# A decoder layer on one core: bank pairs in the other order, the first quarter of x in halves, and banks of their own for the first FFN products

## The chip, the cores and the metric

The kernel runs on one core of a Trainium2 chip. A core has five engines with a queue each: TensorE (PE in the profile, its weight loads PEld), VectorE (DVE), ScalarE (ACT), GpSimd (POOL) and SyncE (SP), which here only issues DMAs. PE multiplies from SBUF into PSUM, which has eight banks of 128 x 512 floats. The metric is the device time of one execution in microseconds. Before the change three runs took 2125.6, 2127.41 and 2127.95 us, a median of 2127.41.

## What is computed

One layer with sparse attention, then a gated feed-forward network (FFN), on x of 512 tokens by 2048 channels in float32:

```python
hn = rmsnorm(x, mix_norm_g)
h = x + nsa_mixer(hn, ...)                 # 16 heads of 128, 4 key/value groups
h = h + swiglu(rmsnorm(h, ffn_norm_g), ffn_w_in, ffn_w_out)   # D_FF = 5632
return rmsnorm(h, final_norm_g)

def nsa_mixer(h, ...):
    proj = h @ w_in                        # q, kc, vc, ks, vs, kw, vw, gates
    ...                                    # compressed, selected and window branches
    o = gates0 * o_c + gates1 * o_s + gates2 * o_w
    return o @ w_out

def swiglu(h, w_in, w_out):
    z = h @ w_in
    a, b = z[..., :D_FF], z[..., D_FF:]
    return (jax.nn.silu(a) * b) @ w_out
```

## The kernel before

**Products.** Every float32 operand is split into a high and a low part (`hi`, `lo`, or a trailing `_h`, `_l`), and a product is three matmuls (`three`, L267 to L269): high by high, high by low, low by high. Making the parts costs one copy on ACT and one subtraction on DVE for each tile: L97 and L98 for weights, L402 and L403 for x.

**Order.** The order of instructions on each engine is that of the Python program; the framework adds the semaphores. An engine works its queue in order, so an instruction that waits holds all behind it. A pool of PSUM or SBUF that is closed gives its place to the next pool opened there, and the first write to such a place waits until the old tile was read for the last time.

**Weights.** `Weights` (L81 to L98) streams granules of 128 x 1024 floats: `load` issues the DMA into one of three `raw` buffers, `split` makes `whi` and `wlo` (four buffers each), `ahead(n)` splits up to n granules past those taken and loads up to three more, `take` hands one out. Its DMAs go on SP's queue, and on POOL's while the heads run.

**The start (L372 to L485).** x comes as four tiles of 128 tokens, each in four quarters of 512 channels. SP loads a weight granule and the even tiles of a quarter, ACT's queue the odd tiles of the first two quarters, and SP all of the last two. PE meanwhile transposes the identity `N_WARM` = 24 times. Then the 16 blocks of the first quarter are transposed (L452) into four banks, ACT and DVE turn each of four banks into `hn_h[k]` and `hn_l[k]` (`scaled_in`), and eight steps follow: `ws` yields after each `three` for one half u of the columns and one channel block k. ACT's squares (L408) and the next quarter's transposes (`chunk`, L398) are mixed in, chunk 4 after step five. This goes on for the four quarters, with q from 0 to 3.

**Bank pairs.** The projections of stage 1 take their two banks in turn from `psx` (2 banks) and `ps1` (6 banks, under three names), by `proj_tiles`. The last pair of the stage is the q of heads 0 and 1 (`q_out`: DVE reads the bank at L319, ACT and DVE write `qh`, `ql` at L292, L293). Then stage 2 opens `ps2` in the place of `ps1`: a score tile of three banks (`s`), one bank for the values (`o`) and two more for projections; its own pairs come in turn from `psx` and `ps2`, beginning with `psx`.

**The heads.** `scores(h, t)` makes the scores of head h and token tile t into the one score tile, takes the maxima (DVE, L800) and the exponentials (ACT, L802). `finish` scales and transposes them in blocks and writes them to DRAM (`d_p`, L817); `fetch` brings them back transposed (`ptr`, L821); `turn` splits them (L838, L842), and `values` multiplies them by v into `o`. Between these steps `pump(h, step)` draws dense work, the projections of later heads, from one stream: steps of 650 ns by the plan's own count (three matmuls of 512 columns) until the count reaches a goal that rises by 20800 ns for each head of twelve steps. The lead in the goal is four steps. Ahead of head 0 there are four calls, one behind each of its scores, at steps 9, 10, 11 and 11.7 of the head before.

**From attention to the FFN.** `out_tiles` and the norms use `psx` and `ps3` (6 banks). Then three plain column blocks of the FFN (N_PLAIN, tiles `pp` of `ps3`), each followed by its gate (`plain_out`: ACT's silu, L1068, or DVE's product, L1066). Then `early` closes both pools and `pf` opens: f0 to f3, two banks each. From there `products(q)` makes seven half-size products per unit (first into f0), and `merge(p)` sums them (L1155 to L1165). After the last unit the second weight matrix follows in units of two row blocks: `W2.take` splits weights, `split_a` the gated activations (`thi`, `tlo`, L1227, L1008), which come from DRAM through buffers `rawx` and `tt` (L1222).

Of the kernel before, what the change touches and what calls it, by code (L numbers as in the profile page):

```python
# [10 lines left out]
F32 = mybir.dt.float32  # L11
# [27 lines left out]
TP_GAP, HN_GAP = 40, 48  # L39
RESYNC = 14  # L40
PT_STEP = 224
SPREAD, N_WARM = UL, 24


def _bucket_onehot():
# [128 lines left out]
def nsa_block(ctx: ExitStack, tc: tile.TileContext, x, rel_bias, mix_g, ffn_g, fin_g, w_in, w_out,  # L174
# [9 lines left out]
    dram = ctx.enter_context(tc.tile_pool(name="dram", bufs=1, space=DRAM))  # L184
    front, early = ctx.enter_context(ExitStack()), ctx.enter_context(ExitStack())
    hnp = front.enter_context(tc.tile_pool(name="hnp", bufs=1))
    psx = early.enter_context(tc.tile_pool(name="psx", bufs=2, space=PSUM))
    specs, specs2, marks, off = granules(w_in, w1k, w1v, w_out, f_in, f_out)
    W = Weights(nc, rawp, convp, specs)
    W.at, W.off = 48, off  # L190
# [159 lines left out]
    with ExitStack() as st1:  # L350
# [2 lines left out]
        turns = iter(range(1000))  # L353

        def proj_tiles(n=2):
            return [(ps1 if next(turns) % 4 > 1 else psx).tile([128, 512], F32, name="proj") for _ in range(n)]

        c0p = st1.enter_context(tc.tile_pool(name="c0p", bufs=1))
        posT = c0p.tile([128, 2, 32], F32, name="posT")
# [2 lines left out]
        with ExitStack() as st0:  # L362
# [7 lines left out]
            ones = xp.tile([128, 128], F32, name="ones")  # L370
            diag = xp.tile([128, NT, 128], F32, name="diag")
            nc.scalar.dma_start(g16, mix_g.rearrange("o (k p) -> (o k) p", p=128))  # L372
            for q in range(4):
                if q < RAW:
                    W.load()
                for t in range(NT):
                    eng = nc.scalar if q < 2 and t % 2 else nc.sync
                    eng.dma_start(xt[t][:, 512 * q:512 * (q + 1)], x[tok(t), 512 * q:512 * (q + 1)])
                if q == 0:
                    act(warm, epsc, AF.Sqrt)  # L380
                if q == 1:
                    nc.sync.dma_start(oh, onehot[:, :UL])
            pool.dma_start(pos[:, 0], pos_k)
# [61 lines left out]
            p = bank([128, KC])  # L445
            nc.tensor.transpose(p, g16, ident[:KC, :KC])
            dve.tensor_copy(gcol, p)
            W.split()
            ps = [bank([128, S]) for _ in range(4)]
            for t in range(NT):  # L450
                for k in range(4):
                    nc.tensor.transpose(ps[k][:, tok(t)], xt[t][:, 128 * k:128 * (k + 1)], ident)  # L452
            for k in range(4):
                scaled_in(k, ps[k])
            ps = proj_tiles()
            for q in range(4):
                it = ws(ps, q, W.take(0))
                next(it)
                if q == 3:
                    factors()  # L460
                W.ahead(1)
                if q == 1:
                    pos_turn()
                    table(0, 512)
                    table(512, UL)
                if q == 2:
                    by_blocks()
                for i in ((0, 1), (2, 3, 4), (5, 6, 7), ())[q]:
                    square(i)
                for _ in range(4):  # L470
                    next(it)
                if q == 3:
                    W.ahead(2)
                for k in range(4 * q + 4, 4 * q + 8):
                    if q < 3:
                        chunk(k)
# [153 lines left out]
    with ExitStack() as st2:  # L630
# [112 lines left out]
        STEPS = 12  # L743

        def pump(h, step):
            at = h + (step + 4) / STEPS
            goal = 20800 * min(at, 13) + 22500 * max(at - 13, 0)
            while done["ns"] < goal:
                c = next(stream, "end")
                if c == "end":  # L750
                    return
                done["ns"] += c or 0
# [118 lines left out]
        for i in range(4):  # L871
            scores(0, 3 - i)
            if i > 1:
                fetch(5 - i, pool)
            if i:
                finish(0, 4 - i)
            pump(-1, min(9 + i, 11.7))
        for h in range(H):
            seq = [(b, kt) for kt in (3, 2, 1, 0) for b in (0, 1)] + [(-1, 0)]
            for i in range(STEPS):  # L880
# [34 lines left out]
    n2_hl = hn_t  # L915
    resid = ctx.enter_context(ExitStack())
    accp = resid.enter_context(tc.tile_pool(name="accp", bufs=1))
    ps3 = early.enter_context(tc.tile_pool(name="ps3", bufs=4, space=PSUM))
    acc = accp.tile([128, NT, D], F32, name="acc")
    spill = 256 * N_SPILL  # L920
    nc.sync.dma_start(acc[:, :, spill:], x[:, spill:].rearrange("(t p) c -> p t c", p=128))
# [18 lines left out]
    with tc.tile_pool(name="n2", bufs=1) as n2:  # L940
# [25 lines left out]
        for t in range(NT):  # L966
# [93 lines left out]

    def plain_out(p, ps):
        E[p] = ep.tile([128, 6, 256], F32, name="E")
        for u in range(2):
            o = gate_out(p)[:, 512 * u:512 * (u + 1)]
            if p % 2:
                dve.tensor_tensor(o, gate_out(p - 1)[:, 512 * u:512 * (u + 1)], ps[u], op=OP.mult)  # L1066
            else:
                act(o, ps[u], AF.Silu)  # L1068
        if p % 2:
            keep_a(p)  # L1070

    def keep_a(p):
        pool.dma_start(d_a[p // 2], gate_out(p))
# [49 lines left out]
    def products(q):  # L1123
        p, u = q // 2, q % 2
        if not u:
            banks[p] = [pf.tile([128, 512], F32, name=f"f{i}").rearrange("p (a c) -> p a c", a=2)
                        for i in range(4)]
# [40 lines left out]
    with tc.tile_pool(name="tmp", bufs=1) as tmp:  # L1168
        todo = sums(tmp)

        def some(n):
            for _ in range(n):
                next(todo, None)

        for i in range(4):
            run(ws(pa, i, gs[i], 256, 512, start=False, of=n2_hl))
            W.ahead(min(i + 1, 3))
            some(1 if i < 3 else 2)
        for p in range(N_PLAIN):
            if p:  # L1180
                pa = [ps3.tile([128, 512], F32, name="pp") for _ in range(2)]
                for i in range(4):
# [8 lines left out]
                    run(ws(pa, i, w, of=n2_hl))  # L1191
            W.ahead(3)
            plain_out(p, pa)
# [91 lines left out]
    merge(NQ // 2 - 1)  # L1285
    front.close()

# [129 lines left out]
            yield  # L1417

    w8, todo = [], iter(())
    n, na, pending = 0, 1, None  # L1420
    for b in range(4):
        units = ORDER[b][:-N_TAIL] if b == 3 else ORDER[b]
        po = [pf.tile([128, 512], F32, name=f"f{i}") for i in range(4)]
        qs = {x: pf.tile([128, 512], F32, name=f"f{i}") for i, x in enumerate(("p1", "p5", "p6", "p7"))}
# [84 lines left out]
```

## Time and profile before

| | before |
|---|---|
| three runs, us | 2125.6, 2127.41, 2127.95 |
| the profiled execution, us | 2127.83 |
| its span, us | 2126.1 |
| mean granted clock of PE | 0.997 |
| matmuls | 14697 |
| DMA, MB | 388.08, mean 183 GB/s |

The span is that of the instructions on the core; the execution's time has 1.7 us around it. In the rows that follow, a row of the timeline has its start, its length, engine, line, operation, the tile written and those read, and in brackets how long the engine had stood idle before and what released it. A matmul's length overlaps the next one's, so the distance of two starts says what one costs: 0.23 us for 512 columns. A row of windows has the stretch, its length, the busy time of PE, PEld, DVE, ACT and POOL with counts, the granted clock of PE (1.00 is full), the busy share of the DMA engines and GB/s.

```profile
PE   9999999999999999999999999999999999999998
DVE  5565777877786466898888888888888777877785
PEclk9999999999999999999999999999999999999999
DMA  7555667666676633444344343443333776878894
```

These are the busy tenths of the span in 40 slices of 53 us. The start is in the first slice, the passage from stage 1 to the heads in the fourth, that to the FFN's products in the seventeenth, and that to the second weight matrix in the thirty-second.

### The profile page before, as it was taken

The numbers are of one execution on the slowest core, as the hardware profiler recorded it, in microseconds if no ns is written. First come the engines' busy times: TensorE is split into PE (matmuls) and PEld (weight loads), VectorE is DVE, ScalarE is ACT, GpSimd is POOL, SyncE is SP. The second block draws the span as 40 slices with busy tenths as digits, with TensorE's granted clock in tenths as the row PEclk, the third lists the DMA queues.
The fourth block names the chain that finished last, engine by engine and source line by source line (L and its number), as shares of the span: only waits on it lengthen the run. The fifth ranks groups of instructions, "written<-read, shape, count | busy, mean of one in ns | idle before, by whom it ended". The sixth has DMA issues, their size and how long they took to land.

```text
span 2126.1 us, 37171 instructions
## 1 busy us (share of the span) xinstructions
PE 2099.3 (99%) x14697; PEld 1947.6 (92%) x14697; DVE 1634.5 (77%) x2670; ACT 932.5 (44%) x1447; POOL 125.8 (6%) x206
## 2 busy tenths in 40 slices
PE   9999999999999999999999999999999999999998
PEld 7898788898989889899999999999999888999996
DVE  5565777877786466898888888888888777877785
ACT  5344455555554334434334343443434444444344
POOL 1000111111111000000000000000000000001000
PEclk9999999999999999999999999999999999999999
DMA  7555667666676633444344343443333776878894
GB/s 228 180 151 151 192 193 201 184 200 188 199 233 203 240 140 109 128 131 129 120 129 129 120 126 123 129 127 122 123 124 122 273 274 213 302 271 309 307 335 143
DMA packets 272635, 388.08 MB, mean 183 GB/s; under 512 B 34155, under 2 KB 204715, under 8 KB 271820
## 3 DMA queue, kind: packets, MB, share of 16 engines
q1 hardware_dynamic: 247660, 279.19, 41.7%
q0 software_dynamic: 22896, 102.31, 13.9%
q10 hardware_dynamic: 1904, 4.20, 0.5%
q8 instruction: 115, 1.88, 0.4%
q14 instruction: 60, 0.49, 0.1%
HBM read 320.52 MB, written 70.36 MB: 184 GB/s over the span
## 4 chain that ended last, share of the span: by engine, by line
PE 68%; DVE 1%; DMA 1%; ACT 1%; issue 0%; ACTq 0%; DVEq 0%
PE f L268 19%; PE f L269 19%; PE f L267 19%; PE proj L267 2%; PE proj L269 2%; PE proj L268 2%; PE pp L267 1%; PE pp L269 1%; PE pp L268 1%; PE po L267 1%; PE po L268 1%; PE po L269 1%; DMA tt<-d_a 1%; PE pp L245 0%; DVE tlo L1008 0%
## 5 line engine op out<-in xcount | busy, mean ns | idle before, releaser
L98 DVE TENSOR_TENSOR wlo<-raw,whi 128x1024 fp32r<-128x1024 f32 (+1 forms) x226 | 270.8, 1200 | 114.5 <-ACT whi L97 114.3
L97 ACT ACTIVATE whi<-raw 128x1024 fp32r<-128x1024 f32 (+1 forms) x226 | 234.4, 1040 | 222.6 <-DVE raw L1008 123.7
L1008 DVE TENSOR_TENSOR tlo<-tt,thi 128x1536 fp32r<-128x1536 f32 (+2 forms) x135 | 197.2, 1460 | 109.2 <-ACT thi L1110 87.2
L267 PE MATMUL f<-hn_h,whi 128*128 128x256 f32 x984 | 272.0, 276 | 0.8 <-ACT E L1068 0.8
L268 PE MATMUL f<-hn_l,whi 128*128 128x256 f32 x984 | 271.9, 276 | 0.0
L269 PE MATMUL f<-hn_h,wlo 128*128 128x256 f32 x984 | 271.9, 276 | 0.0
L1105 ACT ACTIVATE whi<-raw 128x1024 fp32r<-128x1024 f32 x123 | 126.0, 1057 | 293.7 <-DVE raw L1008 283.5
L267 PE MATMUL proj<-hn_h,whi 128*128 128x512 f32 x512 | 204.3, 399 | 0.5 <-ACT hn_h L402 0.5
L268 PE MATMUL proj<-hn_l,whi 128*128 128x512 f32 x512 | 200.9, 392 | 0.3 <-DVE hn_l L403 0.3
L269 PE MATMUL proj<-hn_h,wlo 128*128 128x512 f32 x512 | 200.7, 392 | 0.0
L267 PEld LDWEIGHTS f<-hn_h,whi 128*128 128x128 f32 x984 | 184.8, 188 | 1.2 <-ACT E L1068 1.2
L269 PEld LDWEIGHTS f<-hn_h,wlo 128*128 128x128 f32 x984 | 184.7, 188 | 0.0
L268 PEld LDWEIGHTS f<-hn_l,whi 128*128 128x128 f32 x984 | 184.7, 188 | 0.0
L1110 ACT ACTIVATE thi<-tt 128x1536 fp32r<-128x1536 f32 x82 | 121.9, 1486 | 82.7 <-PE f L268 71.1
L269 PE MATMUL proj<-whi,hn_l 128*128 128x256 f32 (+2 forms) x496 | 146.3, 295 | 2.9 <-DVE hn_l L703 2.9
L1008 DVE TENSOR_TENSOR wlo<-raw,whi 128x1024 fp32r<-128x1024 f32 x123 | 147.1, 1223 | 1.1 <-ACT whi L1105 1.1
L267 PE MATMUL proj<-whi,hn_h 128*128 128x256 f32 (+2 forms) x496 | 146.6, 296 | 0.8 <-ACT hn_h L702 0.8
L268 PE MATMUL proj<-wlo,hn_h 128*128 128x256 f32 (+2 forms) x496 | 145.7, 294 | 0.0
L269 PE MATMUL f<-whi,tlo 128*128 128x512 f32 x320 | 125.0, 391 | 0.6 <-DVE tlo L1008 0.6
L268 PE MATMUL f<-wlo,thi 128*128 128x512 f32 x320 | 125.1, 391 | 0.3 <-DVE wlo L98 0.3
L267 PE MATMUL f<-whi,thi 128*128 128x512 f32 x320 | 124.8, 390 | 0.0
L269 PEld LDWEIGHTS proj<-hn_h,wlo 128*128 128x128 f32 x512 | 96.5, 189 | 21.5 <-DVE wlo L98 0.2
(327 smaller groups left out, 6104.7 us busy)
## 6 DMA issues: line engine op xcount, KB each, us to landing
raw<-in_ffn_w_in SPq DMA_DIRECT2D x135, 512.0 KB, 3.6
raw<-in_ffn_w_out SPq DMA_DIRECT2D x88, 512.0 KB, 6.0
rawx<-in_ffn_w_in SPq DMA_DIRECT2D x41, 512.0 KB, 4.9
rawx<-d_a SPq DMA_DIRECT2D x31, 512.0 KB, 4.9
ah<-d_s POOLq DMA_DIRECT2D x16, 896.0 KB, 7.2
al<-d_s POOLq DMA_DIRECT2D x16, 896.0 KB, 9.5
raw<-in_nsa_w_in SPq DMA_DIRECT2D x24, 512.0 KB, 4.6
raw<-in_nsa_w_in POOLq DMA_DIRECT2D x24, 512.0 KB, 4.8
```

The source lines that it names most:

```text
L97: self.nc.scalar.activation(hi[:, :n], src, AF.Copy)
L98: self.nc.vector.tensor_tensor(lo[:, :n], src, hi[:, :n].bitcast(F32), op=OP.subtract)
L267: mm(o, ah, bh, start=start, stop=False, skip_group_check=True)
L268: mm(o, ah, bl, start=False, stop=False, skip_group_check=True)
L269: mm(o, al, bh, start=False, stop=stop, skip_group_check=True)
L1008: dve.tensor_tensor(o, a, b, op=OP.subtract)
L1105: act(h, r, AF.Copy)
L1110: act(h, ttf, AF.Copy)
```

## The change

- **Start.** The first granule and the first quarter of x are loaded, split, transposed and multiplied in halves of 256 channels: `half(0)`, two steps, `half(1)`, six steps. The odd tiles of the second quarter move from ACT's queue to SP's. `N_WARM` falls from 24 to 20.
- **Bank pairs.** `proj_tiles` gives `ps1` where it gave `psx`, and the other way round.
- **Lead.** In `pump` the lead is five steps up to head 0 and falls evenly to four at head 3. The four calls ahead of head 0 are at steps 8, 9.3, 10.6 and 11.9.
- **FFN banks.** `psx` is closed by itself after the last norm and `pf0` opens in its place, for f0; `ps3` lies at the other end of PSUM, and `pf` has f1 to f3. The gate of a plain block is made half by half, as soon as that half's last matmul is issued (`end`), and the next weights are split ahead of the second half.
- **Last merge.** The second unit's weights and activations are split ahead of the last `merge`, and the loop begins with `na` = 2.

```diff
-SPREAD, N_WARM = UL, 24
+SPREAD, N_WARM = UL, 20
...
-    psx = early.enter_context(tc.tile_pool(name="psx", bufs=2, space=PSUM))
+    firstp = ctx.enter_context(ExitStack())
+    psx = firstp.enter_context(tc.tile_pool(name="psx", bufs=2, space=PSUM))
...
-            return [(ps1 if next(turns) % 4 > 1 else psx).tile([128, 512], F32, name="proj") for _ in range(n)]
+            return [(psx if next(turns) % 4 > 1 else ps1).tile([128, 512], F32, name="proj") for _ in range(n)]
...
-            for q in range(4):
+            first = rawp.tile([128, 1024], F32, name="raw")
+            for a in range(2):
+                w0 = slice(512 * a, 512 * (a + 1))
+                nc.sync.dma_start(first[:, w0].rearrange("p (k c) -> p k c", k=2), specs[0][2][0][2][:, 2 * a:2 * a + 2])
+                for t in range(NT):
+                    eng = nc.scalar if t % 2 else nc.sync
+                    eng.dma_start(xt[t][:, 256 * a:256 * (a + 1)], x[tok(t), 256 * a:256 * (a + 1)])
+                if not a:
+                    act(warm, epsc, AF.Sqrt)
+            W.nd = 1
+            for q in range(1, 4):
                 if q < RAW:
                     W.load()
                 for t in range(NT):
-                    eng = nc.scalar if q < 2 and t % 2 else nc.sync
-                    eng.dma_start(xt[t][:, 512 * q:512 * (q + 1)], x[tok(t), 512 * q:512 * (q + 1)])
-                if q == 0:
-                    act(warm, epsc, AF.Sqrt)
+                    nc.sync.dma_start(xt[t][:, 512 * q:512 * (q + 1)], x[tok(t), 512 * q:512 * (q + 1)])
...
-            W.split()
-            ps = [bank([128, S]) for _ in range(4)]
-            for t in range(NT):
-                for k in range(4):
-                    nc.tensor.transpose(ps[k][:, tok(t)], xt[t][:, 128 * k:128 * (k + 1)], ident)
-            for k in range(4):
-                scaled_in(k, ps[k])
+            W.ncv = W.nt = 1
+            whi, wlo = (convp.tile([128, 1088], F32R, name=f"w{n}")[:, W.at:W.at + 1024] for n in ("hi", "lo"))
+
+            def half(a):
+
+                c = slice(512 * a, 512 * (a + 1))
+                act(whi[:, c], first[:, c], AF.Copy)
+                dve.tensor_tensor(wlo[:, c], first[:, c], whi[:, c].bitcast(F32), op=OP.subtract)
+                p2 = [bank([128, S]) for _ in range(2)]
+                for t in range(NT):
+                    for k in range(2):
+                        nc.tensor.transpose(p2[k][:, tok(t)], xt[t][:, 128 * (2 * a + k):128 * (2 * a + k + 1)], ident)
+                for k in range(2):
+                    scaled_in(2 * a + k, p2[k])
+
+            def first_steps(ps):
+                for a in range(2):
+                    for i in range(4):
+                        u, k = i // 2, 2 * a + i % 2
+                        cs = slice(256 * k + 128 * u, 256 * k + 128 * (u + 1))
+                        three(ps[u], whi[:, cs], wlo[:, cs], hn_h[:, k], hn_l[:, k], k == 0, False)
+                        yield
+                        if not a and i == 1:
+                            half(1)
+
+            half(0)
             ps = proj_tiles()
             for q in range(4):
-                it = ws(ps, q, W.take(0))
-                next(it)
+                it = ws(ps, q, W.take(0)) if q else first_steps(ps)
+                for _ in range(1 if q else 3):
+                    next(it)
...
-                for _ in range(4):
+                for _ in range(4 if q else 2):
                     next(it)
...
-            at = h + (step + 4) / STEPS
+            at = h + step / STEPS
+            at += (4 + min(max(1 - at / 3, 0), 1)) / STEPS
...
-            pump(-1, min(9 + i, 11.7))
+            pump(-1, 8 + 1.3 * i)
...
-    ps3 = early.enter_context(tc.tile_pool(name="ps3", bufs=4, space=PSUM))
+    ps3 = early.enter_context(tc.tile_pool(name="ps3", bufs=4, space=PSUM, side="right"))
...
+        firstp.close()
+        pf0 = ctx.enter_context(tc.tile_pool(name="pf0", bufs=2, space=PSUM))
         pa = [ps3.tile([128, 512], F32, name="pp") for _ in range(2)]
...
+    def f_tile(i):
+        return (pf if i else pf0).tile([128, 512], F32, name=f"f{i}")
...
         products(q)
+    W2.ahead(2)
+    split_a(1)
     merge(NQ // 2 - 1)
...
-    n, na, pending = 0, 1, None
+    n, na, pending = 0, 2, None
```

More of the change, by code (lines that the diff above doesn't have):

```diff
@@ L1062, in plain_out, with end @@
         E[p] = ep.tile([128, 6, 256], F32, name="E")
-        for u in range(2):
+        def end(u):
             o = gate_out(p)[:, 512 * u:512 * (u + 1)]
@@ L1068, in plain_out @@
                 act(o, ps[u], AF.Silu)
-        if p % 2:
-            keep_a(p)
+            if p % 2 and u:
+                keep_a(p)
+        return end
     def keep_a(p):
@@ L1125, in products @@
         if not u:
-            banks[p] = [pf.tile([128, 512], F32, name=f"f{i}").rearrange("p (a c) -> p a c", a=2)
-                        for i in range(4)]
+            banks[p] = [f_tile(i).rearrange("p (a c) -> p a c", a=2) for i in range(4)]
         order = ("p1", "p5", "p2", "p3", "p7", "p6", "p4") if p else ("p1", "p5", "p2", "p7", "p6", "p4", "p3")
@@ L1173, in some @@
                 next(todo, None)
+        end = plain_out(0, pa)
         for i in range(4):
-            run(ws(pa, i, gs[i], 256, 512, start=False, of=n2_hl))
+            run(ws(pa, i, gs[i], 256, 512, start=False, end=end, of=n2_hl))
             W.ahead(min(i + 1, 3))
@@ L1181, in nsa_block @@
                 pa = [ps3.tile([128, 512], F32, name="pp") for _ in range(2)]
+                end = plain_out(p, pa)
                 for i in range(4):
@@ L1190, in nsa_block @@
                         load_unit(2)
-                    run(ws(pa, i, w, of=n2_hl))
+                    run(ws(pa, i, w, end=end, of=n2_hl))
             W.ahead(3)
-            plain_out(p, pa)
         for u in range(2):
@@ L1419, in nsa_block @@
     w8, todo = [], iter(())
-    n, na, pending = 0, 1, None
+    n, na, pending = 0, 2, None
     for b in range(4):
         units = ORDER[b][:-N_TAIL] if b == 3 else ORDER[b]
-        po = [pf.tile([128, 512], F32, name=f"f{i}") for i in range(4)]
-        qs = {x: pf.tile([128, 512], F32, name=f"f{i}") for i, x in enumerate(("p1", "p5", "p6", "p7"))}
+        po = [f_tile(i) for i in range(4)]
+        qs = {x: f_tile(i) for i, x in enumerate(("p1", "p5", "p6", "p7"))}
         first7 = next(j for j in units if j in SEVEN[b])
```

## The prediction

> **What bounds the kernel.** I read the page first (busy time, then the chain that ended last), then the waits of PE, then the timeline around each wait.
>
> ```profile
> PE 2099.3 (99%) x14697; PEld 1947.6 (92%) x14697; DVE 1634.5 (77%) x2670; ACT 932.5 (44%) x1447; POOL 125.8 (6%) x206
> PE 68%; DVE 1%; DMA 1%; ACT 1%; issue 0%; ACTq 0%; DVEq 0%
> ```
>
> PE is busy for 99% of the span, and no other engine has a visible share of the chain. The change takes no matmul of the model away, so it can win only where PE stands still. The waits of PE are few enough to count (engine, tile and line, released by: us in total, times, longest):
>
> ```profile
> PE o L267 <- issue: 3.0, 1, 3.0
> PE proj L269 <- DVE hn_l L703: 2.9, 2, 2.2
> PE s L267 <- DVE yt L319: 1.7, 1, 1.7
> PE tr L452 <- DMA x<-in_x: 1.6, 2, 0.9
> ```
>
> Of these, the second (the reload of heads near 600 us) is not touched: from head 3 on the new lead is the old one, four steps. The other three are addressed, and five waits of 1 us or less whose rows come with their parts. A wait is worth a little more than its idle time, since a matmul after a gap no longer overlaps the one before; below I take starts: the gap between two starts less the usual pitch, 0.23 us for 512 columns and 0.12 for 256 or for the small ones.
>
> **1. The start.** Before:
>
> ```profile
> 1.42 4.56 PE L444 MATMUL tr<-ident 128*128 128x128 f32 x24 [1.42 <-POOL ident masks.py:199]
> 8.79 0.33 PE L452 MATMUL tr<-ident,x 128*128 128x128 f32 x1 [0.61 <-DMA x<-in_x]
> 10.31 0.75 DVE L403 SCALAR_TENSOR_TENSOR hn_l<-tr,gcol,hn_h 128x512 fp32r<-128x512 f32 x1 [2.82 <-ACT hn_h L402]
> 10.33 0.50 PE L267 MATMUL proj<-hn_h,whi 128*128 128x512 f32 x1 [0.45 <-ACT hn_h L402]
> 14.47 0.60 PE L398 MATMUL tr<-ident,x 128*128 128x128 f32 x4
> GB/s 0 0 0 140 207 236 343 312 164 234 388 399 395 378 379 364 376 369 376 365 244 284 348 367 386 382 386 386 396 389 393 377 367 348 347 350 333 121 247 350
> ```
>
> The last row is the DMA view of the first 24 us, 0.6 us a slice. It gives 0.84 MB by 5.4 us and 0.98 MB by 6.0. The first half needs 0.79 MB (0.26 of the granule, 0.52 of x), and the ACT queue mixes some of its second halves in, so I put it at 5.6 to 6.0. From the last tiles' arrival to the first matmul went 10.33 - 8.79 = 1.54 us; with half the transposes I take 1.1, so the first matmul starts near 7.0, not 10.33. DVE's 0.75 us per hn_l holds the first two steps to 8.9; the eight transposes of the second half take 0.9; steps three to five take 3 x 0.69, hn_l[2] and hn_l[3] arriving just ahead. Transposes of chunk 4 come at 11.9 instead of 14.47: 2.57 us. They also need the second quarter of x: 3.15 MB with the two granules, which the row reaches at 12.0. I take 2.2. Bounds: 2.57, and 0 if that quarter lands as late as 14.47 (the trace shows only that it was there by then). The odd tiles of the second quarter change from ACT's queue to SP's, behind granule 1; that is in the 3.15 MB. Later quarters are not needed before q = 1.
>
> The four warm-up transposes removed (24 took 4.56 us) cost nothing, since PE waits for x anyway; if that cover fails it is the clock that is late, a rival below. ACT's two squares of q = 0 still come between hn_h[3] and hn_h[4]; hn_h[4] is needed only in q = 1, some 3.9 us after chunk 4's transposes.
>
> *A rule against it.* The first 24 us move at up to 399 GB/s with DMAs of 256 and 512 KB in flight together. The Trainium skill, "DMA: Bandwidth & Descriptors", Bandwidth, asks for DMAs of 1 MiB and gives 0.95 us for 64 KB against 6.15 us for 1 MB, so about 0.6 us fixed for each DMA, my estimate from the two; five more DMAs would be 3 us if they ran one after the other, and the start would win nothing. Here several queues overlap them, so I don't follow it.
>
> **2. Bank pairs, and more filling behind the first scores.**
>
> ```profile
> 200.56 0.69 DVE L293 TENSOR_TENSOR ql<-yt,qh 128x512 fp32r<-128x512 f32 x1 [0.70 <-ACT qh L292]
> 202.65 0.68 DVE L319 SCALAR_TENSOR_TENSOR yt<-proj,ybc 128x512 f32<-128x512 f32 x1
> 204.03 0.69 DVE L293 TENSOR_TENSOR ql<-yt,qh 128x512 fp32r<-128x512 f32 x1 [0.70 <-ACT qh L292]
> 205.31 0.19 DVE L800 CUSTOM_DVE_ANT_0 cx<-s,biasc 128x31 f32<-128x31 f32 x1 [0.58 <-PE s L269]
> ...
> 201.37 0.39 PE L269 MATMUL proj<-hn_h,wlo 128*128 128x512 f32 x1
> 203.48 0.37 PE L267 MATMUL s<-k0h,qh 128*128 128x288 f32 x1 [1.72 <-DVE yt L319]
> 213.25 0.40 PE L267 MATMUL s<-k0h,qh 128*128 128x288 f32 x1 [0.78 <-DVE mx L800]
> 219.18 0.28 PE L269 MATMUL s<-k0h,ql 128*128 128x256 f32 x1
> 222.50 0.30 PE L267 MATMUL o<-pth,v0h 128*128 128x128 f32 x1 [3.05 <-issue]
> ...
> 212.49 19.49 SPq L817 DMA_DIRECT2D d_p<-p  x17
> 217.09 0.77 POOL L821 DMA_DIRECT2D ptr<-d_p  x1 [17.07 <-DMA d_p<-p]
> 222.10 0.51 ACT L838 ACTIVATE pth<-ptr 128x128 fp32r<-128x128 f32 x2 [4.23 <-DMA ptr<-d_p]
> ```
>
> Head 0's q was ready at 201.25 (first row); the scores waited until 203.48 for DVE's read of head 1's bank, because the score tile lies on ps1's banks. With the pairs turned, that last pair is in psx, and the scores start at 201.6: 2.11 - 0.23 = 1.88 us. But DVE's maxima still stand behind the second ql (204.03 to 204.72), so they start only 0.6 earlier than 205.31; the second scores, which overwrite what the maxima read, then make PE wait about 1.0 us. From there the softmax chain is some 0.9 us earlier (0.6 on DVE, and the rest since it then waits less for PE). The wait at 213.25 (0.78 idle) goes, filled by one extra step. The long one is a chain through DRAM: write at 212.49, fetch at 217.09, ACT at 222.10. Its 9.6 us I leave, so the values start near 221.6. Meanwhile, by the goals of pump, 16 steps of 0.69 have been done rather than 14. Together 0.9 + 2 x 0.69 = 2.25; I take 2.2. Bounds: all three gaps gone, 1.88 + 0.78 + 3.20 = 5.9; and -0.7, if the granule that the ninth step loads, now ahead of the second fetch on POOL's queue, holds the chain by its 0.52 MB at 246 GB/s (2.1 us; the rate is in the rows below), with the 1.4 of the steps kept. What is late next is the same fetch, with a gap of about 2.85 us. The first steps now write psx just after its own last pair; its first bank had been read before 200.56, so nothing waits. The lead given up by head 3 moves work, and adds none.
>
> *The clock.* After that gap the clock falls:
>
> ```profile
> 222.00:224.00 2.00, 1.50 (x6) 1.26 (x7) 1.39 (x7) 0.51 (x2) 0.42 (x2) 0.86 0.91 306
> 224.00:226.00 2.00, 2.00 (x8) 1.63 (x7) 1.29 (x6) 0.56 (x2) 0.68 (x1) 0.50 0.83 246
> 226.00:228.00 2.00, 2.00 (x8) 1.64 (x8) 1.05 (x4) 1.75 (x7) 0.00 (x0) 0.79 0.67 205
> ...
> 611.98 0.39 PE L269 MATMUL proj<-whi,hn_l 128*128 128x256 f32 x1 [2.15 <-DVE hn_l L703]
> 613.00:615.00 2.00, 2.00 (x10) 1.89 (x10) 0.69 (x8) 1.80 (x8) 0.00 (x0) 0.50 0.83 224
> ```
>
> The granted clock is the seventh figure: 2 x (0.14 + 0.50 + 0.21) = 1.7 us lost. At 612 a gap of 2.15 us did the same, so I expect 2.85 to do it too and count nothing. The Trainium skill, "TensorE: Matmul & The Clock Gate", Part 1, has a free-running window of 3.4 us and half the clock after an idle one; by that a gap of 2.85 would keep the clock. The trace disagrees with it at 2.15.
>
> **3. Own first banks in the FFN.**
>
> ```profile
> 879.15 0.39 PE L269 MATMUL pp<-hn_h,wlo 128*128 128x512 f32 x1
> 880.31 0.39 PE L267 MATMUL f<-hn_h,whi 128*128 128x256 f32 x1 [0.77 <-ACT E L1068]
> ```
>
> 1.16 - 0.23 = 0.93 us. The first product now writes pf0, on psx's idle banks; its 12 matmuls cover 1.37 us, and ACT's gate, still ending about 880.3, frees the others. The gates themselves are issued earlier, but ACT reaches the last no sooner. Bounds 0 and 0.93; I take 0.9.
>
> **4. The second unit's splits before the last merge.**
>
> ```profile
> 1661.68 1.14 DVE L1011 TENSOR_TENSOR E<-E,f 128x512 f32<-128x512 f32 x2 [2.08 <-ACT E L1155]
> 1665.93 1.22 DVE L98 TENSOR_TENSOR wlo<-raw,whi 128x1024 fp32r<-128x1024 f32 x1
> 1667.07 1.22 DVE L1008 TENSOR_TENSOR tlo<-tt,thi 128x1024 fp32r<-128x1024 f32 x1
> ...
> 1666.52 0.39 PE L267 MATMUL f<-whi,thi 128*128 128x512 f32 x1
> 1667.20 0.50 PE L268 MATMUL f<-wlo,thi 128*128 128x512 f32 x1 [0.29 <-DVE wlo L98]
> 1668.34 0.50 PE L269 MATMUL f<-whi,tlo 128*128 128x512 f32 x1 [0.63 <-DVE tlo L1008]
> ...
> 1720.81 0.38 PE L267 MATMUL f<-thi,ah 128*128 128x256 f32 x1
> 1722.20 0.39 PE L268 MATMUL f<-tlo,ah 128*128 128x256 f32 x1 [1.01 <-DVE tlo L1008]
> ```
>
> DVE's merge (1661.68 to 1665.9) stood ahead of wlo and tlo. Now wlo falls before 1661, where DVE idles, and tlo ends near 1663.5, so both gaps go: 0.45 + 0.91 = 1.36. The merge ends some 1.5 later; its readers come far later. At 1722.20 the gap is 1.39 - 0.12 = 1.27, behind a load of `tt` among saturated DMAs. Weights for the next units now load some 6 us earlier, which helps, while PE arrives 1.4 earlier, which hurts: from -1.4 to 1.27, and I take 0.6.
>
> **Sum.** 2.2 + 2.2 + 0.9 + 1.4 + 0.6 = 7.3 us from the profiled execution's 2127.83 (span 2126.1, 1.7 around it), which is 0.4 above the median of the runs: **2120.5**.
>
> **Rivals.**
> - *The clock holds.* The new gap of 2.85 falls across two windows, or the threshold lies above it: 1.7 more, 2118.8. For it: the gap is shorter than 3.2. Against: 612. Chance 0.15.
> - *Handed back.* The stage entry wins nothing because the fetches meet the earlier weight load, and the gap at 1722 takes back part 4's 1.4: only 2.2 + 0.9 stay, 2124.7. For it: 0.9 and more of the DMA share in both places. Chance 0.14.
> - *The start doesn't do what it says.* With 20 transposes the clock falls back while PE waits for x (1.7), and the second quarter is late (the 2.2 gone): 2124.4. Against: before, a start with two waits for x kept it. Chance 0.06.
> - *Slower.* POOL's weight load waits for its raw buffer in front of the second fetch. The longest such wait is
>
> ```profile
> POOL raw L81 <- DVE wlo L98: 240.2, 44, 11.2
> ```
>
> so up to 11.2 us for the values of head 0, and one more half-clock window, 1.7: 2120.5 + 12.9 = 2133.4. It turns the sign from about 5 us of standing on (2127.4 - 2120.5 - 1.7). Against: DVE splits that granule soon after 212.49, while POOL still waits to fetch until 217.09. Chance 0.05.
>
> **Chances and range.** The forecast has 0.60, with 2118 to 2123 of its own. A measurement of this kernel can tell about 0.2%, 4.25 us. Faster: the forecast and the first rival, 0.74 (a little of the forecast lost at its edge, less than rounding); within 0.2%: the next two and that edge, 0.21; slower 0.05. The range, 2117.0 to 2125.0, holds the first three rivals' times and leaves out the outer bounds.
>
> **What would show it.** First proj matmul near 7.0 and chunk 4's transposes near 12; the first score's matmul 0.2 us after the last proj, a new gap of about 1 us before the second scores, 16 steps before the first values, and a gap of 2.85 there; no gap at the first f matmul nor in the second unit of the last stage; a smaller one in place of 1722's. It is wrong if PE gains new waits in the heads, or if the first chunks wait for x.

## The result, and the profile after

The changed kernel is slower: a median of 2135.26 us over seven runs (2132.43 to 2136.7) against 2127.84 us for the kernel before, run seven times beside it (2125.6 to 2132.09). The ratio is 1.0034, with a 95% interval of 1.0025 to 1.0043. Forecast were 2120.5 us, with 2117 to 2125 as the range. The profiled execution of the changed kernel has a span of 2134.6 us against 2126.1, and a mean granted clock of 0.996 against 0.997.

The busy times, from the page of the changed kernel, show next to nothing:

```profile
PE 2105.0 (99%) x14693; PEld 1950.8 (91%) x14693; DVE 1635.3 (77%) x2671; ACT 933.5 (44%) x1448; POOL 126.3 (6%) x206
```

DVE and ACT do the same work within a microsecond. The waits of PE (us in total, times, longest) tell more. At their head stand two: the first isn't in the list of the kernel before, and the second has 1.4 us there:

```profile
PE o L268 <- ACT pth L867: 4.6, 3, 2.3
PE o L269 <- DVE ptl L871: 4.3, 9, 1.0
```

PE now waits for the turned scores, `pth` and `ptl`, ahead of the products with v (tile `o`). Where these waits lie is seen in PE's timeline of the changed kernel, of which these are rows of the start, and the larger waits of the entry, of the first heads and of the last stage:

```profile
7.22 0.33 PE L467 MATMUL tr<-ident,x 128*128 128x128 f32 x1 [0.24 <-DMA x<-in_x]
8.55 0.50 PE L268 MATMUL proj<-hn_h,whi 128*128 128x512 f32 x1 [0.67 <-ACT hn_h L410]
13.66 0.60 PE L406 MATMUL tr<-ident,x 128*128 128x128 f32 x4
...
205.30 0.40 PE L268 MATMUL s<-k0h,qh 128*128 128x288 f32 x1 [0.87 <-DVE mx L829]
220.21 0.30 PE L268 MATMUL o<-pth,v0h 128*128 128x128 f32 x1 [2.06 <-issue]
...
244.08 0.50 PE L268 MATMUL o<-pth,v0h 128*128 128x512 f32 x1 [2.25 <-ACT pth L867]
245.42 0.71 PE L269 MATMUL o<-ptl,v0h 128*128 128x512 f32 x1 [0.84 <-DVE ptl L871]
277.17 0.50 PE L268 MATMUL o<-pth,v0h 128*128 128x512 f32 x1 [1.12 <-ACT pth L867]
277.97 0.50 PE L269 MATMUL o<-ptl,v0h 128*128 128x512 f32 x1 [0.30 <-DVE ptl L871]
...
308.99 0.51 PE L268 MATMUL o<-pth,v0h 128*128 128x512 f32 x1 [1.27 <-ACT pth L867]
309.79 0.50 PE L269 MATMUL o<-ptl,v0h 128*128 128x512 f32 x1 [0.30 <-DVE ptl L871]
...
1681.79 0.50 PE L270 MATMUL f<-whi,tlo 128*128 128x512 f32 x1 [0.18 <-DVE tlo L1039]
1687.88 0.38 PE L270 MATMUL f<-thi,al 128*128 128x256 f32 x1 [0.53 <-DVE al L1039]
1731.05 0.39 PE L269 MATMUL f<-tlo,ah 128*128 128x256 f32 x1 [1.01 <-DVE tlo L1039]
```

The entry to the heads (205.30, 220.21) looks as forecast. The rows from 244.08 to 309.79 are in heads 0 to 2, where the forecast has none. Counted by starts, as the prediction counts, these six cost 2.41, 1.12, 1.28, 0.58, 1.44 and 0.58 us; with two more, of 1.14 at 233.76 and 0.53 at 299.62, that makes 9.1.

The same places can be compared by the starts of their matmuls. In the table are the times before, and below it how much later each kernel reaches that place (the experiments follow; the end of a head is its last matmul with v; each row is from one profiled execution, so that a few tenths mean nothing; the start varies more, since the rows after, 1, 4 and 5 have the same start and bank pairs and their first scores lie up to 1.8 us apart).

| | first proj | first score | end of head 0 | end of head 2 | first plain FFN block | first f | last matmul |
|---|---|---|---|---|---|---|---|
| before, us | 10.33 | 203.48 | 246.88 | 306.41 | 811.46 | 880.31 | 2115.97 |
| after | -1.79 | -2.70 | +4.49 | +9.41 | +9.76 | +8.83 | +8.81 |
| 1 after, old lead | -1.94 | -1.69 | -0.22 | +0.13 | +0.99 | +0.05 | -0.54 |
| 2 before, new lead | +0.09 | +0.07 | +6.32 | +9.73 | +10.03 | +10.02 | +8.48 |
| 3 before, bank pairs | +0.33 | -1.58 | +0.73 | +0.58 | +1.06 | +1.06 | -0.24 |
| 4 after, lead of four | -2.64 | -3.33 | -1.97 | -1.64 | -0.35 | -1.29 | -1.26 |
| 5 after, lead of five throughout | -1.57 | -1.54 | +5.22 | +12.0 | +47.17 | +46.23 | +47.46 |

The changed kernel is 2.70 us ahead at the first score and 9.41 behind at the end of head 2: it loses 12.1 us in three heads of the sixteen. The waits are 9.1 of these; the other part is the clock (windows of the changed kernel, columns as before):

```profile
220.00:222.00 2.00, 1.79 (x8) 1.45 (x9) 1.68 (x7) 0.31 (x2) 0.00 (x0) 0.91 0.96 318
...
244.00:246.00 2.00, 1.08 (x3) 0.67 (x4) 1.97 (x3) 0.03 (x1) 0.76 (x1) 0.89 0.28 69
246.00:248.00 2.00, 2.00 (x6) 1.58 (x5) 1.31 (x2) 1.15 (x2) 0.00 (x0) 0.50 0.65 184
248.00:250.00 2.00, 2.00 (x8) 1.58 (x7) 1.13 (x8) 1.44 (x6) 0.00 (x0) 0.76 0.37 108
308.00:310.00 2.00, 0.71 (x2) 0.39 (x3) 1.38 (x3) 2.00 (x4) 0.00 (x0) 1.00 0.86 207
310.00:312.00 2.00, 2.00 (x10) 1.92 (x10) 1.94 (x5) 0.41 (x1) 0.46 (x1) 0.60 0.09 23
312.00:314.00 2.00, 2.00 (x12) 2.00 (x11) 1.37 (x7) 1.88 (x7) 0.29 (x1) 0.55 0.49 96
```

The first fall, at the entry, was there before. Two are new, behind the waits at 244 and at 309: 2 x (0.11 + 0.50 + 0.24) = 1.7 us and 2 x (0.40 + 0.45) = 1.7 us. With 9.1 that makes 12.5. The entry's own two waits behind the first score are shorter than before, 3.3 us by starts where the kernel before has 4.2, so 11.6 of the 12.1 lost are accounted for.

**Why `pth` is late.** ACT and DVE of the changed kernel in head 0, ahead of the wait at 244.08:

```profile
241.93 0.63 ACT L293 ACTIVATE qh<-yt 128x512 fp32r<-128x512 f32 x1 [4.36 <-DVE yt L320]
242.47 1.04 ACT L97 ACTIVATE whi<-raw 128x1024 fp32r<-128x1024 f32 x1
243.41 0.61 ACT L867 ACTIVATE pth<-ptr 128x512 fp32r<-128x512 f32 x1
```

```profile
237.08 1.23 DVE L98 TENSOR_TENSOR wlo<-raw,whi 128x1024 fp32r<-128x1024 f32 x1 [1.85 <-ACT whi L97]
238.22 0.68 DVE L871 TENSOR_TENSOR ptl<-ptr,pth 128x512 fp32r<-128x512 f32 x1
...
240.21 1.11 DVE L844 STREAM_TRANSPOSE p<-p 128x896 f32<-128x896 f32 x1
```

And ACT and DVE of the kernel before in the same head:

```profile
236.97 0.62 ACT L838 ACTIVATE pth<-ptr 128x512 fp32r<-128x512 f32 x1
241.60 0.63 ACT L292 ACTIVATE qh<-yt 128x512 fp32r<-128x512 f32 x1 [4.01 <-DVE yt L319]
```

```profile
236.15 0.69 DVE L842 TENSOR_TENSOR ptl<-ptr,pth 128x512 fp32r<-128x512 f32 x1 [1.42 <-ACT pth L838]
...
238.15 1.11 DVE L815 STREAM_TRANSPOSE p<-p 128x896 f32<-128x896 f32 x1
239.18 1.18 DVE L98 TENSOR_TENSOR wlo<-raw,whi 128x1024 fp32r<-128x1024 f32 x1
```

Before, the second `pth` came at 236.97, ahead of the end of q (`qh`), and DVE did the first `ptl` and `finish` (with the transpose, 238.15) ahead of the weights' `wlo`. After, the dense work has been drawn further, by a lead of nearly one more twelfth of a head. DVE reaches `wlo` first and stands idle 1.85 us, because ACT's `whi` is not there; `ptl` and `finish` stand behind it. On ACT the second `pth` stands behind `qh` and the next `whi` and comes at 243.41, 6.4 us later than before. Nothing was added; the same instructions stand in another order.

**Why one step is enough.** A granule serves eight steps of the plan's count, and a unit (a pair of heads' q, a pair of k, a pair of v) has four granules: 32 steps x 650 ns = 20800 ns, exactly what the goal rises by in a head. `pump` is called at the end of each of the twelve steps, and stops as soon as its count reaches the goal. With a lead of four the goals at steps 2, 5, 8 and 11 are (2 + 4)/12 x 32 = 16 steps of the plan, then 24, 32 and 40: each on the edge of a granule. The next `take`, and with it the next split, is then drawn only by the call of the following step, behind that step's turn and `finish`. Any lead above four asks for a part of a step beyond the edge, and the split moves ahead of them. The changed kernel is above four until head 3, and it is there that it loses.

### The profile page after: what moved, and what is told of

It reads as the page before. It is cut to its first block, busy times and chain, and to the rows that moved or that the text cites. A ratio compares the mean times of both kernels' runs of the same rounds, so it can differ in the third digit from the quotient of the medians.

```text
span 2134.6 us, 37173 instructions
## 1 busy us (share of the span) xinstructions
PE 2105.0 (99%) x14693; PEld 1950.8 (91%) x14693; DVE 1635.3 (77%) x2671; ACT 933.5 (44%) x1448; POOL 126.3 (6%) x206
## 4 chain that ended last, share of the span: by engine, by line
PE 67%; DMA 1%; DVE 1%; ACT 1%; issue 0%; ACTq 0%; DVEq 0%
PE f L269 19%; PE f L270 19%; PE f L268 19%; PE proj L268 2%; PE proj L270 2%; PE proj L269 2%; PE pp L269 1%; PE pp L270 1%; PE pp L268 1%; PE po L270 1%; PE po L269 1%; PE po L268 1%; DMA tt<-d_a 1%; PE pp L246 0%; DMA acc<-d_a 0%
```

## The experiments

Each kernel was run beside the kernel before on the same chip. Ratios are against it, with their 95% interval. There were ten runs of each, but four of experiments 2, 11 and 12, and two of 5.

**1. The changed kernel with the old lead, whole.** In `pump` and ahead of head 0:

```diff
-            at = h + step / STEPS
-            at += (4 + min(max(1 - at / 3, 0), 1)) / STEPS
+            at = h + (step + 4) / STEPS
...
-            pump(-1, 8 + 1.3 * i)
+            pump(-1, min(9 + i, 11.7))
```

> The changed kernel with pump as it was: a lead of four steps throughout and the old four calls ahead of head 0. Theory A (the lead puts splits and q's ends ahead of the turns in ACT's and DVE's queues, and PE waits in heads 0 to 2): the 9.3 us of new losses between 195 and 350 us go, about 2124 (2127.8 less 0.9 at the start, 1.5 at the scores, 0.9 in the FFN, 0.2 at the end). Theory B (the bank pairs' order makes the heads wait): stays near 2135.

Measured: 2125.94 us (ten runs) against 2128.60 (25 runs), a ratio of 0.9985 (0.9975 to 0.9994). The loss of heads 0 to 2 is gone (the table: -1.69 at the first score, +0.13 at the end of head 2), and so is the wait for `pth`. This version is ahead of both kernels: 3.2 us below the kernel before (0.0015 x 2128.6; 1.3 to 5.3), and by the two ratios 10 below the changed one.

**2. The kernel before with the new lead alone.** The two edits of experiment 1 the other way round, in the kernel before.

> The kernel before with only the new lead and the new four calls. Theory A: slower by 8 to 12 us, 2136 to 2140, with the waits of PE on pth and ptl in heads 0 to 2. Theory B: 2125 to 2128.

Measured: 2137.28 us, 1.0039 (1.0024 to 1.0054). The lead, with its four calls, makes the whole loss: +6.32 at the end of head 0, +9.73 at the end of head 2, and little after it.

**3. The kernel before with the bank pairs turned.**

```diff
-(ps1 if next(turns) % 4 > 1 else psx)
+(psx if next(turns) % 4 > 1 else ps1)
```

> The kernel before with only the bank pairs in the other order. Theory A: the wait before the first scores (1.9 us) goes and about 1 us comes back before the second, so 2126 to 2128. Theory B: 2134 to 2138, with the waits on pth and ptl in heads 0 to 2.

Measured: 2127.20 us, 0.9992 (0.9983 to 1.0001). The first score is 1.9 us earlier against the first proj, as worked out, but three waits follow it:

```profile
206.42 0.40 PE L267 MATMUL s<-k0h,qh 128*128 128x288 f32 x1 [0.87 <-DVE mx L800]
212.72 0.40 PE L267 MATMUL s<-k0h,qh 128*128 128x288 f32 x1 [0.75 <-DVE mx L800]
222.03 0.45 PE L267 MATMUL o<-pth,v0h 128*128 128x128 f32 x1 [3.12 <-issue]
```

By starts 1.03 + 0.92 + 3.29 = 5.24 us, where the kernel before has 1.89 + 0.95 + 3.22 = 6.06. So 0.8 is left of the 1.9; the rest waits for DVE's maxima and for the way through DRAM.

**4. The changed kernel with a lead of four, and the fill behind the first scores kept.** Ahead of head 0 the calls reach a step further than the old ones, and from head 0 on all is as before.

```diff
+            at = h + (step + 4) / STEPS
...
+            pump(-1, 9 + 1.3 * i)
```

> The changed kernel with the new goals for the four calls ahead of head 0 but a lead of four steps from head 0 on. If the falling lead in heads 0 to 2 is what costs, 2123 to 2125. If the filling behind the first scores is what costs (the earlier weight load ahead of the fetches on POOL's queue), most of the loss stays: 2132 to 2136.

Measured: 2126.27 us, 0.999 (0.998 to 0.9999). It loses nothing behind head 0, so it is the lead inside the heads that costs, not the calls ahead of them. It isn't faster than experiment 1 either: the four calls by themselves bought nothing that can be told. They draw the work earlier, but not more of it: 14 steps (42 matmuls of `proj`) stand between the first score and the first values, as in the kernel before and in experiment 1. The changed kernel has 16, and the two more come by its lead in the first steps of head 0.

**5. A lead of five throughout.**

```diff
+            at = h + (step + 5) / STEPS
```

> The changed kernel with a lead of five steps in all heads. Theory A1 (a pair of heads' projections is 32 steps, a head's goal rises by 32 steps, so a lead above four puts a q's end ahead of the last turns of the same head, in every head): the 2 us that heads 1 and 2 lost are lost in the later heads too, 12 x 2 us more than the changed kernel, about 2159, with waits on pth in heads 3 to 14. Theory A2 (the weight loads pulled ahead meet the first fetches; only the entry suffers): 2133 to 2137.

Measured: 2175.75 us, 1.0222 (1.0201 to 1.0242). It is more than expected: it loses some 4.1 us in each of heads 3 to 9, and 2.4 in heads 10 and 11. In the first seven the clock falls once each (1.7 us), in the other two it doesn't, which is the difference. The cost doesn't belong to the entry, nor to the step from five to four; it is there wherever the lead is above four. PE's list is headed by the wait of the changed kernel, multiplied:

```profile
PE o L268 <- ACT pth L866: 15.1, 12, 2.2
```

Its granted clock is 0.989, where experiment 1 has 0.998: some 0.009 x 2126 = 19 us of the loss, by this estimate, are falls of the clock, most of them behind these waits.

**6. A lead of three.**

```diff
+            at = h + (step + 3) / STEPS
...
+            pump(-1, 10 + 1.3 * i)
```

> The changed kernel with a lead of three steps in all heads, the four calls ahead of head 0 with the goals that the change gave them. A1: q's ends stand behind all turns, as with four, so 2124 to 2128. If instead more lead as such costs and less helps, 2120 to 2123; if too little lead leaves PE without work behind the scores, above 2130.

Measured: 2132.53 us, 1.0015 (1.0006 to 1.0025), a miss. Heads 0 to 5 run half a microsecond ahead of the kernel before, as expected, but by the end of head 15 it is 7.2 us behind, and among its waits are some for the reloaded heads, this one for instance:

```profile
PE proj L268 <- DMA hn_l<-d_o: 2.0, 1, 2.0
```

It is at 618.37, at the reload of finished heads from DRAM; that the dense work gets there with less in hand is a guess, which no run took apart. Of the 7.2 us, 6.2 come in heads 12 to 15. So a lead below four costs at the far end, and one above four at once.

**7. The ends of the q and k pairs held back.** The changed kernel, with the work that closes a pair (`q_out`, `k_out`: `yt`, `qh`, `ql`) put off until the next turn has been issued.

```diff
+        late = []
+        def later(end):
+            return lambda u: late.append((end, u))
...
-            end = q_out(ps, h0)
+            end = later(q_out(ps, h0))
...
```

> The changed kernel with its falling lead, but the ends of q and k pairs (the reads of their banks on DVE and ACT) are held back until the next turn was issued; matmuls and weight loads keep their order. A1: the waits on pth and ptl in heads 0 to 2 go, 2124 to 2128. A2, or the earlier splits and loads alone: stays at 2132 to 2136.

Measured: 2131.11 us, 1.0011 (1.0001 to 1.002): of the 0.49% between experiment 1 and the changed kernel about half is left, and the time lies between the two forecasts. The wait for `pth` is gone from PE's list, but one for the maxima stands at its head, with one for `ptl` behind it:

```profile
PE s L268 <- DVE mx L840: 5.4, 5, 1.5
```

Holding back the ends isn't enough: the weight splits still stand ahead of `ptl` (in head 0 `wlo` at 236.74, again behind 1.85 us of standing idle). But in head 0 the second of the ends still stands ahead of the next maxima too (`yt` at 245.43, the maxima from 247.43), so this run doesn't divide the loss. The next two take the two causes apart.

**11 and 12. Leads of 4.10 and 4.15.** Both with the old calls ahead of head 0. At 4.10 the splits come a step early, while the end of q still falls behind the turn. By the count, the end of a pair's first bank, at the 28th of 32 steps, is passed at 12 x 17550/20800 - 6 = 4.125, so at 4.15 the ends come early too.

```diff
+            at = h + (step + 4.1) / STEPS
```

> The changed kernel with the old calls ahead of head 0 and a lead of 4.10 steps in all heads. Against 4 (2125.9) this moves the weight splits that fall on a goal's edge ahead of a turn, and no end of a q. If the ends alone cost (E): 2125 to 2128. If the splits ahead of the turns cost (S): 1 to 2 us in each of 15 heads, 2140 to 2156.

> The same with a lead of 4.15: beyond 4.125 the 28th of a pair's 32 steps is drawn in step six of the head, and with it the first end of a q comes ahead of the turn of step seven; nothing else moves against 4.10. E: about 2 us more in each of the heads with a q or k pair, 2148 to 2158. S: within 3 us of the kernel at 4.10.

Measured: 2151.65 us, 1.0101 (1.0084 to 1.0118), and 2152.78 us, 1.0105 (1.0086 to 1.0124). A tenth of a step of lead, 0.1 x 20800/12 = 173 ns of the plan's count, costs some 25 us against experiment 1 (the ratios differ by 0.0116); the next twentieth adds 1.1, which is within the intervals. So at these leads the splits carry nearly all of it. From 4.15 to five the ratio rises as much again, by 0.0117 or 25 us. About 13 of these are the clock (0.989 where 4.15 has 0.995, over 2152 us). By the same count the last split of a pair, ahead of its 29th step, passes the turn from a lead of 4.5 on (`whi` at 242.47 in head 0 of the changed kernel), and the pair's second end from 4.625 on; neither was tried alone. In DVE's order of instructions 4.10 differs from experiment 1 in where the splits stand; head 1 in experiment 1, and then at 4.10:

```profile
268.10 1.11 DVE L843 STREAM_TRANSPOSE p<-p 128x896 f32<-128x896 f32 x1
269.13 1.18 DVE L98 TENSOR_TENSOR wlo<-raw,whi 128x1024 fp32r<-128x1024 f32 x1
...
275.94 0.08 DVE L828 DVE_READ_ACCUMULATOR2_ANT mx<- 128x1 f32 x1
```

```profile
269.86 1.23 DVE L98 TENSOR_TENSOR wlo<-raw,whi 128x1024 fp32r<-128x1024 f32 x1 [1.85 <-ACT whi L97]
271.00 0.68 DVE L870 TENSOR_TENSOR ptl<-ptr,pth 128x512 fp32r<-128x512 f32 x1
273.19 1.11 DVE L843 STREAM_TRANSPOSE p<-p 128x896 f32<-128x896 f32 x1
...
279.90 0.08 DVE L828 DVE_READ_ACCUMULATOR2_ANT mx<- 128x1 f32 x1
```

`wlo` stands behind the transpose in the one and ahead of `ptl` and the transpose in the other, with the 1.85 us of standing idle. The maxima of the following tile end 279.90 - 275.94 = 3.96 us later. Of these, 1.82 are left from head 0, which ends that much later at 4.10; the rest is this head's, and PE waits for the maxima. At 4.10 PE's list is headed by waits for `mx` and `ptl`; at 4.15 the end of q has moved ahead of the turn as well, and the first wait is again `pth`, as in the changed kernel:

```profile
PE s L268 <- DVE mx L828: 10.8, 13, 1.0
PE o L269 <- DVE ptl L870: 8.8, 18, 1.0
```

```profile
PE o L268 <- ACT pth L866: 10.7, 10, 1.4
```

**8. The start in halves alone.** The hunks of the start in the kernel before, the 24 warm-up transposes kept.

> The kernel before with only the start in halves (24 warm-up transposes kept). By the trace of the change the first chunk's transposes come 0.8 us earlier, so 2126.5 to 2127.5; by the prediction's 2.2 us, 2125.5. If the second quarter of x is late, as in e1 where PE waited 1.2 us for it, no gain: 2127.5 to 2129.

Measured: 2128.16 us against 2128.82, 0.9999 (0.999 to 1.0009): no difference. The first proj matmul is 1.67 us earlier, the first score 0.39, each in one profile.

**9. The FFN's own first banks alone**, with the gates half by half. The two were not taken apart.

```diff
+        return (pf if i else pf0).tile([128, 512], F32, name=f"f{i}")
```

> The kernel before with only the banks of their own for the first FFN products and the gates half by half. The gap of 0.93 us before the first f matmul goes and nothing comes back: 0.9 us less than before (2127.9 beside 2128.8). If the gap only moves to another bank, no change.

Measured: 2127.06 us against 2128.97, 0.999 (0.998 to 0.9999). Over the place itself, from the first plain block to the first f, it gains 0.94 us (62.25 us where the kernel before takes 63.19), and this holds within 0.01 us in every profile with or without this part.

**10. The splits ahead of the last merge alone.**

```diff
+    W2.ahead(2)
+    split_a(1)
     merge(NQ // 2 - 1)
...
-    n, na, pending = 0, 1, None
+    n, na, pending = 0, 2, None
```

> The kernel before with only the second unit's splits ahead of the last merge. The prediction's account: 1.4 to 2.0 us less. The account of the changed kernel's trace (DVE still has the merge to do, and the next units wait for it and for the load of the first form): 0 to 0.5 us less.

Measured: 2127.44 us against 2128.97, 0.9994 (0.9985 to 1.0003). Between the first product of the second weight matrix and the last matmul its profile takes 453.48 us, 1.42 less than that of the kernel before. But four other kernels with the old last merge take 453.05 to 453.62 there (part 4 below), so this is no gain of the edit that can be told.

## Why the prediction was wrong

**The step that failed** is the last sentence of part 2: "The lead given up by head 3 moves work, and adds none." It costed the lead by its matmuls, and those were indeed only moved. But a step that is drawn also issues its weights' `whi` on ACT (1.04 us) and `wlo` on DVE (1.23), or the end of a pair, and these went on in-order queues ahead of `ptl`, `pth` and `finish`, which PE needs next. Experiment 2 puts the whole loss on the lead (+9.7 us by the end of head 2; experiment 1 without it has +0.1), experiment 5 shows that it is paid in each head with a lead above four, and experiment 11 that the place of the splits costs by itself, with no end moved. That the ends have a part too is seen in the changed kernel's rows (`pth` behind `qh`) and suggested by experiment 7; how its loss divides between the two isn't shown. That "from head 3 on the new lead is the old one" was right, and from there on nothing more is lost. The closing words, that it is wrong "if PE gains new waits in the heads", named the sign; no rival had the mechanism. The slower rival had POOL's weight load in front of the second fetch. It did not come: the values of head 0 start at 220.21, 2.3 us earlier than before.

**Part 1, the start.** Mis-sized. The 2.57 us of chunk 4's transposes became 14.47 - 13.66 = 0.8. The first proj matmul came at 8.55, not 7.0: the last tile of the first half landed at 7.2 rather than by 6.0, and `hn_h` took 8.55 - 7.22 = 1.33 from there, not 1.1. By the runs of experiment 8 the start is worth 0.2 us (2.1 gained to 1.9 lost) where 2.2 were counted. The estimate from the Trainium skill, "DMA: Bandwidth & Descriptors", Bandwidth, that the start would win nothing, is nearer to this than mine; but its reason, a fixed cost for each DMA, isn't shown by the runs. In the nine profiles with the halved start the first proj matmul lies between 7.62 and 8.76, in the five with the old one between 10.33 and 10.66; of this, 0.39 us are left at the first score in experiment 8. In the profile of experiment 1 PE waits for the second quarter of x, near 14 us, the zero bound of this part:

```profile
14.21 0.33 PE L406 MATMUL tr<-ident,x 128*128 128x128 f32 x1 [0.33 <-DMA x<-in_x]
```

**Part 2, the bank pairs.** The scores came 1.9 us earlier, a gap of 0.87 before the second scores and a shorter one before the values, as described. In the changed kernel the entry even won more than was counted: by starts, its waits from the first scores to the first values fall from 6.04 to 3.26 us, 2.8 for the 2.2 (whose sum, 0.9 + 2 x 0.69, is 2.28 and not 2.25). But that includes the two more steps, and they come by the lead in head 0, the same lead whose cost follows in heads 0 to 2. Without it, in experiment 1, 4.94 us of waits are left, a gain of 1.1; the bank pairs alone give 0.8 by the gaps, and 1.7 by the runs (3.6 gained to 0.2 lost).

**Part 3, the FFN.** Right: 0.93 worked out, 0.94 measured, and nothing was handed back.

**Part 4, the last merge.** Both gaps near 1667 are gone, as predicted (1.36). In the changed kernel others of 0.34 and 0.70 us by starts came at 1681.79 and 1687.88, and the gap at 1722, counted on for 0.6, is still 1.25 (1731.05). Between the two places of experiment 10 the changed kernel gains 0.2 us, experiment 1 gains 0.8 and experiment 10 1.42, of 2.0. That is against the one profile of the kernel before, with 454.90 us for the stretch. Experiments 2, 3, 8 and 9 have the old last merge too and take 453.05, 453.60, 453.14 and 453.62, and none of them has the gap of 1722. So the 0.6 was counted on a wait of that one profile, and no gain of this part is shown. Why the new gaps are larger in the changed kernel wasn't tried.

**The clock.** At the entry it fell as forecast, behind a gap of 2.06 us. That is luck in part: in experiments 8 and 11 gaps of 3.1 and 3.0 us at the same place had no fall behind them, nor had gaps of 2.36 and 2.25 in experiments 2 and 5. What no term held is that the new waits cost it twice more, 3.4 us.

**In sum.** 7.3 us were forecast from parts 1 to 4; the same parts without the lead, and so without the two more steps of part 2, give 3.2 (experiment 1), and the lead takes some 10.

## What to carry to other kernels

When filler work is drawn from a stream between the steps of a latency chain, cost the instructions that a drawn step puts on the other engines' queues, and not only its matmuls: write down, engine by engine, what then stands ahead of the chain's next instruction. Look at where the drawing stops against the edges of the stream: here goals lay exactly on the granules' edges, and an amount far too small to matter by the plan moved a split in every granule. A lead that has been fitted is best tried on both sides before it is shaped.

## What the runs showed of the hardware

**The clock's windows.** In the changed kernel the falls of the granted clock begin, by the rows of windows, at about 221.64, 245.56, 310.40 and 624.44 us, and each lasts 3.4 us (248.96 is the end of the second, for instance). Their distances are 7.01, 19.0 and 92.0 times 3.413 us, so they lie on one grid, wherever the gaps end. That agrees with the Trainium skill, "TensorE: Matmul & The Clock Gate", Part 1, which gives a free-running window of 3413 ns. It disagrees with the idle window that the page asks for: in the window that ends at 310.40, PE stood idle for 1.27 + 0.30 us, 46% of it, and the clock fell. The gaps of 1.12 and 0.30 us near 277 lie in the window from 276.28 to 279.69 with 0.89 + 0.30 = 1.19 us, 35%, and it held. But the share of idle time alone doesn't set the limit. In experiment 11 a window of its grid (120 windows lie between its end and the fall near 630.5) was busy for 1.62 of 3.41 us, 53% idle, and the clock held:

```profile
217.47:220.88 3.41, 1.62 (x9) 1.29 (x9) 1.73 (x5) 0.59 (x4) 2.54 (x4) 1.00 0.98 273
220.88:224.30 3.42, 2.18 (x10) 1.83 (x11) 1.96 (x8) 0.51 (x2) 0.00 (x0) 1.00 1.00 325
```

Over all the traces, from 10 us on, every fall from the full clock came behind a window with 44% of idling or more, and windows with up to 55% held. What decides in between isn't shown.

**The same gap can cost or not.** At the reload of the heads the changed kernel has a gap of 2.06 us and experiment 1 one of 2.16. In experiment 1 the clock held:

```profile
610.00:612.00 2.00, 0.90 (x8) 0.69 (x6) 1.92 (x6) 1.06 (x2) 0.00 (x0) 1.00 1.05 340
612.00:614.00 2.00, 0.94 (x6) 0.77 (x6) 2.00 (x2) 0.00 (x0) 0.00 (x0) 1.00 1.03 346
```

Its only fall ahead of the last matmul begins near 222.98; the grid from there has an edge at 612.10, inside the gap from 610.90 to 613.06, so that PE idles for 1.2 us of the one window (35%) and 1.1 of the other (0.96 and the 0.17 at 614.19). In the changed kernel the gap of 2.06 lies with 1.7 us in the window that ends at 624.44, 49%, and the clock fell. So a gap of this size can cost 1.7 us more or less, and these two fit with where it lies on the grid.
